# The rows of four RMS norms: column products and a power, or one fp32 product and ScalarE's reciprocal root

## The chip, the cores and the metric

The kernel runs on one core of one Trainium2 chip. The core has TensorE (matrix products, PE in the profile, its weight loads PEld), VectorE (DVE), ScalarE (ACT), GpSimd (POOL) and the queue engine SyncE (SP), which issues most of the transfers. Each engine works through its own queue in order and waits on semaphores. TensorE writes into PSUM, eight banks of 128 partitions by 512 fp32 values; everything else lies in SBUF. The metric is the time of one execution on the device in microseconds (us), as the median of several runs.

## The reference

The program is one decoder layer on 512 tokens of width 1024, all in fp32: a SwiGLU feed-forward block (ffn1), a mixer of state-space heads and differential attention (mix), cross-attention into a memory of 256 tokens (cross), a second feed-forward block (ffn2) and a final norm. What matters here is that each of the four blocks begins with an RMS norm of the 512 tokens:

```python
def rms_norm(x, w):
    x32 = x.astype(jnp.float32)
    y = x32 * lax.rsqrt(jnp.mean(x32 * x32, axis=-1, keepdims=True) + EPS)
    return y.astype(x.dtype) * w

x = x + 0.5 * swiglu(rms_norm(x, norm_ffn1_w[l]), ...)
x = x + hybrid_mixer(rms_norm(x, norm_mix_w[l]), ...)
x = x + memory_cross_attention(rms_norm(x, norm_cross_w[l]), rms_norm(mem, norm_mem_w[l]), ...)
x = x + 0.5 * swiglu(rms_norm(x, norm_ffn2_w[l]), ...)
```

EPS is 1e-6 and the mean runs over 1024 values. So each norm needs, for every token, the reciprocal root of the mean square.

## The kernel before

The state x lies transposed: eight tiles of 128 features (partitions) by 512 tokens (columns). Weights come from memory in tiles of 128 x 1024 (wr, six buffers), and every fp32 operand of a large product is split into a high part (wh, h; ScalarE copies it to the format fp32r) and a low part (wl, l; VectorE subtracts), with three buffers each; a product is then three fp32r products, high by high, high by low, low by high. The two feed-forward blocks also use Strassen-like block products of 256 columns (`quad`, line 252: banks qa, qe, qb). TensorE's queue is therefore a long row of such products, and the splits are what ScalarE and VectorE mostly do.

The norm's factor is per token, that is per column of these tiles. A gain per feature is applied when a tile is split or scaled; the factor per token is multiplied in as a row of 512 values that stands in all 128 partitions. Class `Stat` makes it. `add` squares each of the eight x tiles (ScalarE) and adds them up (VectorE, tile nacc). `finish` (lines 404 to 413) then takes these steps:

- four column products, each with a block of 128 tokens of nacc as weights and a column of ones moving, so that each token's sum lands in a column (tile nps, 128 x 4);
- on VectorE the division by 1024 and EPS (nv), on GpSimd the power -0.5 (ncol, line 379);
- after some microseconds of other TensorE work (`yield apart`), four products that spread the column into a row over all partitions, with the column broadcast as weights and the identity moving (tile nrow);
- a ScalarE copy of that row into SBUF (tile row).

What uses the row: at ffn1 the gate of the first hidden tiles and the scaled tiles fe and fo; at mix eight tiles hf (line 425), each split into hnh and hnl, which all projections of the mixer read, the first being the query product pq; at cross the query tiles cqf (line 1131); at ffn2 the gates (line 453). ffn2 also needs the factor as a column, for tokens on partitions (col4 and ncol4, lines 1385 and 1386).

The order in which instructions are written is set by `Order`: it counts TensorE's time with every product, runs the dense work (generators that yield after each group of products) and puts in side chains when their counted time has come; `finish` is such a chain. SyncE's and GpSimd's queues keep that written order; on the other engines a scheduler may move instructions that do not depend on each other. Around the mix norm the dense work is the memory's keys (bank pck, eight products of 24 steps), at cross the first query products (pcq), at ffn2 the first quad. GpSimd's queue also holds transfers that add one weight tile onto another in memory (isum, wsum), so what stands behind the power there waits for it.

ScalarE keeps one table of functions at a time; a function from another table needs an ACT_TABLE_LOAD first. The kernel before loads four times: at the start, before the first Silu, before the first Exp, and before the Silu of ffn2.

Of the kernel before, what the change touches and what calls it, by code (L numbers as in the profile page):

```python
# [11 lines left out]
F32 = mybir.dt.float32  # L12
# [5 lines left out]
P = 128  # L18
# [81 lines left out]
def body(tc, a, dbg=None):  # L100
# [31 lines left out]
    def aux(s, shape=(P, T)):  # L132
        return aux_p.tile(list(shape), F32, tag="aux", name=nm(s))
# [9 lines left out]
    def mm(out, w, x, start, stop):  # L143
        od.t += (1 if w.dtype == R32 else 4) * (x.free_size() + 8) / 2400
        newest_mm[:] = [nc.tensor.matmul(out, w, x, start=start, stop=stop).ins]  # L145
# [213 lines left out]
    ones = cp.tile([P, P], F32, name="ones")  # L359
    V.memset(ones, 1.0)  # L360
    mhalf = cp.tile([P, 4], F32, name="mhalf")
    S.activation(mhalf, ones[:, :4], AF.Copy, scale=-0.5)
    ones_r = cp.tile([P, P], R32, name="ones_r")
    V.tensor_copy(ones_r, ones)
# [17 lines left out]
    def row_of(col, nb):  # L382
# [3 lines left out]
                mm(pr[:, b * P : (b + 1) * P], col[:, b : b + 1].to_broadcast([P, P]), ident, True, True)  # L386
        return pr

    class Stat:
        def __init__(self, n_tok=T):  # L390
            self.n = n_tok
            self.acc = None
            self.row = None

        def add(self, xk):
            if self.acc is None:
                self.acc = s2("nacc", shape=(P, self.n))
                S.activation(self.acc, xk, AF.Square)
            else:
                sq = s2("nsq", shape=(P, self.n))  # L400
                S.activation(sq, xk, AF.Square)
                V.tensor_tensor(self.acc, self.acc, sq, ALU.add)

        def finish(self, apart=2.5):
            nb = self.n // P
# [11 lines left out]

    def normed(st, c, dst):

        yield from st.finish()  # L420
        hf = {}
        for k in range(KT + 1):
            if k < KT:
                hf[k] = s2("hf")
                V.scalar_tensor_tensor(hf[k], x[k], par[:, c + k : c + k + 1], st.row, ALU.mult, ALU.mult)
            if k > 0:
                dst.append(split("hn", hf.pop(k - 1)))
                yield 1.6
# [139 lines left out]
    start.extend(last)  # L568
    with tc.issue_after(start[0]):
        for k in range(KT):  # L570
            st1.add(x[k])
    st_mix, h = Stat(), []

    def beside(ti):
# [3 lines left out]
            od.spawn(memory_prep(hm, 2.5), 10.0)  # L578

    def fin1(o):  # L580
        st_mix.add(x[o])
        if o == KT - 3:
            od.spawn(normed(st_mix, C_MIX, h), 3.0)
            od.spawn(block_sums_in_dram(), 60.0)

    od.spawn(st1.finish(), 18.0)
    od.add(ffn1(h1, wa_s, fin1, beside))


# [501 lines left out]
    def upd_c(o, po):  # L1091
        V.tensor_tensor(x[o], x[o], po, ALU.add)
        h_c.append(make_h(o, C_CROSS))
        st_c.add(x[o])
        dump(f"x2_{o}", x[o])
        if o == KT - 1:
            h.clear()
            od.spawn(st_c.finish(), 3.0)

    hm, hm2 = [], []  # L1100
    od.add(memory_keys())
# [72 lines left out]
    def upd_2(o, po):  # L1174
        V.tensor_tensor(x[o], x[o], po, ALU.add)
        gain = par[:, C_FFN2 + o : C_FFN2 + o + 1]
        if o % 2:
            h, l = split("hm", x[o], gain)
            half["12"], half["22"] = hl((h, l), slice(0, H)), hl((h, l), slice(H, T))
            xs_2.append(block_sums(o - 1, C_FFN2, dict(half), even.pop()))  # L1180
        else:
            half["11"] = [s2("h11" + p_, R32, (P, H)) for p_ in "hl"]
            split_into(*half["11"], x[o][:, :H], gain)
            even.append(scaled(o, C_FFN2))
        st_2.add(x[o])
# [306 lines left out]
```

## Time and profile before

| | |
|---|---|
| median of 3 runs | 1308.36 us (1307.47 to 1309.42) |
| the profiled execution | 1306.71 us, of it span 1304.7 us |
| granted TensorE clock | 0.998 of full speed |
| TensorE busy | 1292.8 us, 99% of the span |
| VectorE, ScalarE, GpSimd busy | 969.6, 695.3, 108.9 us |
| the norms' first column product starts at | 25.2, 355.6, 849.8, 971.8 us |

The span is what the profiler saw of the program; the execution's own time has some 2 us around it. A row of the timeline gives start, duration, engine, line, operation, the tile written and the tiles read, the shape, the count, and in brackets how long the engine sat idle before it and what ended that. "issue" means that the profile shows no reason. TensorE's matmuls overlap and their ends are modelled, so distances between starts are the better measure there. An fp32 product shows two records, an fp32r product one.

### The profile page before, as it was taken

The page shows a single profiled execution, that of the slowest core. Times are in us where ns is not written, and L with a number is a line of the kernel's source. Part 1 is how long each engine was busy: PE and PEld are TensorE (multiplying, and loading weights), DVE is VectorE, ACT ScalarE, POOL GpSimd, SP SyncE. Part 2 cuts the span into 40 slices and gives each one's busy share as a digit, 9 for nine tenths or more (in the row PEclk, how much of TensorE's full clock was granted, in tenths as well). Part 3 has the DMA queues.
Part 4 walks back from the last instruction along what each step waited for, and adds up shares of the span by engine and source line. Part 5 has one row for each costly group of instructions (what it writes and reads, how often), then busy time and mean ns, then how long its engine had stood idle before and what let it go on. Part 6 is the DMA issues. An engine that isn't in the chain of part 4 may idle for free.

```text
span 1304.7 us, 20807 instructions
## 1 busy us (share of the span) xinstructions
PE 1292.8 (99%) x8108; PEld 1150.9 (88%) x8108; DVE 969.6 (74%) x1520; ACT 695.3 (53%) x1183; POOL 108.9 (8%) x127
## 2 busy tenths in 40 slices
PE   9999999999999999999999999999999999999997
PEld 7889999999987788887888888888899999989995
DVE  6886888788884787548877796656677878877886
ACT  6444654556553666336564564434465645555564
POOL 1010010000010011200101012020011000000001
PEclk9999999999999999999999999999999999999999
DMA  8156667767664434953468379594239875655662
GB/s 310 49 192 170 191 166 196 186 182 195 186 232 151 129 90 118 265 182 93 117 182 246 105 174 260 188 225 143 69 106 253 223 229 168 191 201 172 191 204 91
DMA packets 69729, 229.03 MB, mean 176 GB/s; under 512 B 8616, under 2 KB 12176, under 8 KB 69280
## 3 DMA queue, kind: packets, MB, share of 16 engines
q1 hardware_dynamic: 52832, 176.26, 38.7%
q0 software_dynamic: 13056, 44.65, 18.9%
q10 hardware_dynamic: 3744, 6.82, 1.7%
q8 instruction: 63, 1.03, 0.3%
q14 instruction: 34, 0.28, 0.1%
HBM read 225.53 MB, written 50.91 MB: 212 GB/s over the span
## 4 chain that ended last, share of the span: by engine, by line
PE 90%; issue 6%; DVE 2%; ACT 1%; POOL 1%; POOLq 0%; ACTq 0%; DVEq 0%
PE qb L252 15%; PE pm L145 10%; PE qa L252 10%; PE qe L252 10%; PE pxbc L145 5%; PE pcq L145 3%; PE pz L145 3%; PE po L145 3%; PE ob L1258 3%; PE pv L145 3%; PE oa L1258 2%; PE pq L145 2%; PE oe L1258 2%; PE pk L145 2%; PE pa L145 2%
## 5 line engine op out<-in xcount | busy, mean ns | idle before, releaser
L154 ACT ACTIVATE wh<-wr 128x1024 fp32r<-128x1024 f32 (+2 forms) x323 | 329.3, 1022 | 355.6 <-issue 95.7
L155 DVE TENSOR_TENSOR wl<-wr,wh 128x1024 fp32r<-128x1024 f32 (+2 forms) x323 | 379.7, 1178 | 144.6 <-ACT wh L154 138.6
L145 PE MATMUL pxbc<-hnh,wh 128*128 128x512 f32 x128 | 52.9, 413 | 0.0
L252 PE MATMUL qb<-s24h,wl 128*128 128x256 f32 x184 | 52.2, 284 | 0.2 <-DVE wl L155 0.2
L252 PE MATMUL qb<-s24h,wh 128*128 128x256 f32 x184 | 52.4, 285 | 0.0
L252 PE MATMUL qb<-s24l,wh 128*128 128x256 f32 x184 | 52.2, 284 | 0.0
L252 PE MATMUL qb<-s31h,wh 128*128 128x256 f32 x184 | 52.2, 283 | 0.0
L252 PE MATMUL qe<-s31h,wh 128*128 128x256 f32 x184 | 52.1, 283 | 0.0
L252 PE MATMUL qb<-s31l,wh 128*128 128x256 f32 x184 | 52.1, 283 | 0.0
L252 PE MATMUL qe<-s24l,wh 128*128 128x256 f32 x184 | 52.1, 283 | 0.0
L252 PE MATMUL qe<-s24h,wh 128*128 128x256 f32 x184 | 52.1, 283 | 0.0
L252 PE MATMUL qb<-s31h,wl 128*128 128x256 f32 x184 | 52.1, 283 | 0.0
L252 PE MATMUL qe<-s31l,wh 128*128 128x256 f32 x184 | 52.1, 283 | 0.0
L252 PE MATMUL qe<-s24h,wl 128*128 128x256 f32 x184 | 52.1, 283 | 0.0
L252 PE MATMUL qe<-s31h,wl 128*128 128x256 f32 x184 | 52.1, 283 | 0.0
L145 PE MATMUL pxbc<-hnh,wl 128*128 128x512 f32 x128 | 50.2, 392 | 0.0
L145 PE MATMUL pxbc<-hnl,wh 128*128 128x512 f32 x128 | 49.9, 390 | 0.0
L754 ACT ACTIVATE ec<-ec,mn 128x512 f32<-128x512 f32 (+3 forms) x64 | 35.5, 556 | 25.7 <-DVE mn L753 25.6
L252 PE MATMUL qa<-h11h,wh 128*128 128x256 f32 x152 | 43.1, 283 | 0.0
L252 PE MATMUL qa<-h11h,wl 128*128 128x256 f32 x152 | 43.0, 283 | 0.0
L252 PE MATMUL qa<-h11l,wh 128*128 128x256 f32 x152 | 43.0, 283 | 0.0
L860 DVE SCALAR_TENSOR_TENSOR conv<-pxbc,par,conv 128x511 f32<-128x511 f32 (+2 forms) x48 | 35.8, 746 | 6.5 <-ACT conv L857 5.7
(490 smaller groups left out, 4171.0 us busy)
## 6 DMA issues: line engine op xcount, KB each, us to landing
wr<-in_f2q SPq DMA_DIRECT2D x44, 512.0 KB, 4.2
wr<-in_f1q SPq DMA_DIRECT2D x40, 512.0 KB, 4.5
isum<-in_f2q SPq DMA_DIRECT2D x22, 512.0 KB, 5.3
wr<-isum SPq DMA_DIRECT2D x22, 512.0 KB, 4.2
wr<-in_f1o SPq DMA_DIRECT2D x20, 512.0 KB, 3.9
wsum<-in_f2b SPq DMA_DIRECT2D x20, 512.0 KB, 6.6
wr<-wsum SPq DMA_DIRECT2D x20, 512.0 KB, 4.3
wr<-in_f1q POOLq DMA_DIRECT2D x16, 512.0 KB, 5.7
```

The lines of the kernel that those rows point to most:

```text
L145: newest_mm[:] = [nc.tensor.matmul(out, w, x, start=start, stop=stop).ins]
L154: S.activation(hi, src, AF.Copy),
L155: V.tensor_tensor(lo, src, hi.bitcast(F32), ALU.subtract),
L252: newest_mm[:] = [nc.tensor.matmul(out, a_[:, wc], b_, start=first and f == 0 and kp == 0 and j == 0, stop=kp == n - 1 and j == 2, skip_gr ...
L754: S.activation(ec[:, :n], ec[:, :n], AF.Exp, bias=mn, scale=-1.0, accum_out=sm[c][:, i : i + 1])
L860: V.scalar_tensor_tensor(y[:, d:], ps[:, : T - d], par[:, cw + j : cw + j + 1], y[:, d:], ALU.mult, ALU.add)
L1258: newest_mm[:] = [nc.tensor.matmul(ps, a_[:, ts], b_[:, ws], start=first and k == 0 and j == 0, stop=k == n - 1 and j == 2, skip_group_che ...
```

## The change

For the four norms of 512 tokens the column products, the power and the spreading products go. The memory's norm and the state-space groups' norms keep theirs.

- The sums go with a minus sign: the last `add` of a norm computes -nacc - sq in one three-operand VectorE instruction. (At mix the last tile added is the sixth, since the tiles come in the order 6, 7, 4, 5.)
- `root_row`: one fp32 product with a 128 x 128 tile of ones as weights and nacc moving gives every token's sum as a row in all partitions at once (nps, now 128 x 512). ScalarE takes the reciprocal root of its absolute value (scale and eps_root bring in EPS and the factor; the result is half the wanted one, divided by 1024), then squares it into a second tile. VectorE multiplies this by the sum and then, in the second instruction, completes a Newton step and the factor.
- `finish_row` is that chain. At ffn2 `finish_both` adds, 16 us of counted time later, four transposes of the row and a VectorE copy of one column out of each, which gives the column that col4 and ncol4 are made from.
- At the start one small ScalarE instruction with the reciprocal root stands ahead of the tile mhalf, so that the first table load brings the table with this function.

```diff
+    eps_root = cp.tile([P, 1], F32, name="eps_root")
+    V.memset(eps_root, 4.0 * D * D * EPS)
+    S.activation(mhalf, ones[:, :4], AF.Abs_reciprocal_sqrt)
     S.activation(mhalf, ones[:, :4], AF.Copy, scale=-0.5)
...
+    def root_row(sums, r, w, sign):
+
+        ps = aux("nps")
+        with behind(list(newest_mm)):
+            mm(ps, ones, sums, True, True)
+        S.activation(r, ps, AF.Abs_reciprocal_sqrt, bias=eps_root, scale=4.0 * D * sign)
+        S.activation(w, r, AF.Square, scale=2.0 * D)
+        V.scalar_tensor_tensor(w, ps, sign * D * EPS, w, ALU.add, ALU.mult)
+        V.scalar_tensor_tensor(r, w, -3.0 * D * sign, r, ALU.add, ALU.mult)
+
...
-        def add(self, xk):
+        def add(self, xk, last=False):
...
-                V.tensor_tensor(self.acc, self.acc, sq, ALU.add)
+                if last:
+                    V.scalar_tensor_tensor(self.acc, self.acc, -1.0, sq, ALU.mult, ALU.subtract)
+                else:
+                    V.tensor_tensor(self.acc, self.acc, sq, ALU.add)
+
+        def finish_both(self, apart):
+            yield from self.finish_row()
+            yield apart
+            nb = self.n // P
+            pt = aux("pcol")
+            for b in range(nb):
+                transpose(pt[:, b * P : (b + 1) * P], self.row[:, b * P : (b + 1) * P])
+            self.col = small("ncol", nb, bufs=6)
+            V.tensor_copy(self.col, pt.rearrange("p (a b) -> p a b", b=P)[:, :, 0])
+
+        def finish_row(self):
+            self.row = s2("row")
+            root_row(self.acc, self.row, s2("nsq"), -1)
+            yield 0.0
...
     def normed(st, c, dst):
 
-        yield from st.finish()
+        yield from st.finish_row()
...
-        st_mix.add(x[o])
+        st_mix.add(x[o], o == KT - 3)
...
-    od.spawn(st1.finish(), 18.0)
+    od.spawn(st1.finish_row(), 18.0)
...
-            od.spawn(st_c.finish(), 3.0)
+            od.spawn(st_c.finish_row(), 3.0)
...
-            od.spawn(st_2.finish(8.0), 7.5)
+            od.spawn(st_2.finish_both(16.0), 7.5)
```

On TensorE the change stands in the same places as the column products did. At ffn1 (pa are the first four hidden tiles, hm the scaled x) the queue holds before:

```order
L145 MATMUL pa_280<-hmh_194,wal_199 128x512
L145 MATMUL nps_365<-ones,nacc_210 128x1 x4
L145 MATMUL pa_277<-hmh_202,wah_206 128x512
L145 MATMUL pa_277<-hml_203,wah_206 128x512
L145 MATMUL pa_277<-hmh_202,wal_207 128x512
```

and with the change:

```order
L145 MATMUL pa_283<-hmh_197,wal_202 128x512
L145 MATMUL nps_370<-nacc_213,ones 128x512
L145 MATMUL pa_280<-hmh_205,wah_209 128x512
L145 MATMUL pa_280<-hml_206,wah_209 128x512
L145 MATMUL pa_280<-hmh_205,wal_210 128x512
```

Four one-column products became one of 512 columns at the same place; the nrow x4 that stood twelve rows further, ahead of the first pg, is gone. The same holds for the other three norms; at ffn2 four pcol transposes are new, within the second quad's first block product.

On VectorE at mix (hf are the scaled tiles, hnl their low parts, wl the low parts of the weights, wdts a small tile) the queue holds before:

```order
L377 TENSOR_SCALAR nv_4098<-nps_4093 128x4
L155 TENSOR_TENSOR wl_4218<-wr_4215,wh_4217 128x1024
L425 SCALAR_TENSOR_TENSOR hf_4140<-x_79,par,row_4138 128x512
L425 SCALAR_TENSOR_TENSOR hf_4142<-x_79,par,row_4138 128x512
L155 TENSOR_TENSOR hnl_4145<-hf_4140,hnh_4144 128x512
L425 SCALAR_TENSOR_TENSOR hf_4157<-x_80,par,row_4138 128x512
L155 TENSOR_TENSOR wl_4254<-wr_4251,wh_4253 128x1024
L155 TENSOR_TENSOR hnl_4160<-hf_4142,hnh_4159 128x512
L425 SCALAR_TENSOR_TENSOR hf_4184<-x_80,par,row_4138 128x512
L648 TENSOR_TENSOR wdts_4456<-wdt_4454,wdts_4456 128x8x16
L155 TENSOR_TENSOR wl_4297<-wr_4294,wh_4296 128x1024
```

and with the change, behind the first Newton pass (nsq) and wdts, which stand ahead of these rows:

```order
L400 SCALAR_TENSOR_TENSOR row_4088<-nsq_4089,row_4088 128x512
L456 SCALAR_TENSOR_TENSOR hf_4096<-x_79,par,row_4088 128x512
L456 SCALAR_TENSOR_TENSOR hf_4098<-x_79,par,row_4088 128x512
L155 TENSOR_TENSOR wl_4253<-wr_4250,wh_4252 128x1024
L155 TENSOR_TENSOR hnl_4101<-hf_4096,hnh_4100 128x512
L456 SCALAR_TENSOR_TENSOR hf_4119<-x_80,par,row_4088 128x512
L155 TENSOR_TENSOR hnl_4122<-hf_4098,hnh_4121 128x512
L456 SCALAR_TENSOR_TENSOR hf_4147<-x_80,par,row_4088 128x512
L155 TENSOR_TENSOR hnl_4150<-hf_4119,hnh_4149 128x512
L456 SCALAR_TENSOR_TENSOR hf_4174<-x_81,par,row_4088 128x512
L155 TENSOR_TENSOR wl_4288<-wr_4285,wh_4287 128x1024
```

The third weight split of these rows (wl_4297 before, wl_4288 now) moved behind one more hf and one more hnl, and two Newton passes stand ahead of all of it.

On ScalarE at ffn2 (qa, qe, qb are the quad's banks, p and u copies of them, gate the first gated tile) the queue holds before:

```order
L298 ACTIVATE qb_10094<-qa_10092 128x512
L306 ACTIVATE p_2030_10161<-qe_10093 128x512
L154 ACTIVATE wh_10223<-wr_10087 128x1024
L154 ACTIVATE wh_10262<-wr_10090 128x1024
L314 ACTIVATE u_2033_10192<-qb_10094 128x512
L154 ACTIVATE wh_10290<-wr_10085 128x1024
L413 ACTIVATE row_10255<-nrow_10250 128x512
L154 ACTIVATE wh_10343<-wr_10327 128x1024
L454 ACT_TABLE_LOAD
L454 ACTIVATE gate_10319<-gate_10319 128x512
```

and with the change:

```order
L298 ACTIVATE qb_10073<-qa_10071 128x512
L154 ACTIVATE wh_10201<-wr_10066 128x1024
L397 ACT_TABLE_LOAD
L397 ACTIVATE row_10131<-nps_10133,eps_root 128x512
L398 ACTIVATE nsq_10132<-row_10131 128x512
L306 ACTIVATE p_2024_10139<-qe_10072 128x512
L314 ACTIVATE u_2027_10170<-qb_10073 128x512
L154 ACTIVATE wh_10233<-wr_10069 128x1024
L154 ACTIVATE wh_10261<-wr_10064 128x1024
L485 ACT_TABLE_LOAD
L485 ACTIVATE gate_10290<-gate_10290 128x512
```

Table load, root and square stand ahead of the copies p and u, and the split wh of the fourth product (wh_10262 before, wh_10233 now) moved behind u. Table loads are eight in all instead of four: one more at mix, two more at cross (one ahead of the root, one ahead of the next Exp) and one more at ffn2.

More of the change, by code (lines that the diff above doesn't have):

```diff
@@ L570, in body @@
         for k in range(KT):
-            st1.add(x[k])
+            st1.add(x[k], k == KT - 1)
     st_mix, h = Stat(), []
@@ L1093, in upd_c @@
         h_c.append(make_h(o, C_CROSS))
-        st_c.add(x[o])
+        st_c.add(x[o], o == KT - 1)
         dump(f"x2_{o}", x[o])
@@ L1184, in upd_2 @@
             even.append(scaled(o, C_FFN2))
-        st_2.add(x[o])
+        st_2.add(x[o], o == KT - 1)
         dump(f"x3_{o}", x[o])
```

## Prediction, made before the changed kernel was run

> **What bounds the kernel now.** I read the page first (busy shares and chain), then the waits by engine, then the timeline around the four norms.
>
> ```profile
> span 1304.7 us, 20807 instructions
> PE 1292.8 (99%) x8108; PEld 1150.9 (88%) x8108; DVE 969.6 (74%) x1520; ACT 695.3 (53%) x1183; POOL 108.9 (8%) x127
> ...
> PE 90%; issue 6%; DVE 2%; ACT 1%; POOL 1%; POOLq 0%; ACTq 0%; DVEq 0%
> ...
> PE ptk L149 <- ACT of L810: 0.6, 1, 0.6
> ```
>
> TensorE works 99% of the span and makes 90% of the chain that ends last; in the list of waits its longest after the start is 0.6 us. So nearly every microsecond taken off TensorE's queue comes off the end, and work on the other engines is free until it makes TensorE wait. The change has to be priced as TensorE's time first, and as the lateness of what TensorE reads second. I call the four norms by their stages: ffn1, mix, cross, ffn2.
>
> **What is taken off TensorE.** Around the ffn1 norm:
>
> ```profile
> 25.20 0.94 PE L145 MATMUL nps<-ones,nacc 128*128 128x1 f32 x8
> ...
> 26.33 0.40 PE L145 MATMUL pa<-hml,wah 128*128 128x512 f32 x1
> ...
> 28.64 0.39 PE L145 MATMUL pa<-hmh,wal 128*128 128x512 f32 x1
> 28.87 1.05 PE L145 MATMUL nrow<-ident,ncol 128*128 128x128 f32 x8
> 29.68 0.48 PE L145 MATMUL pg<-hmh,wh 128*128 128x512 f32 x1
> 29.99 0.39 PE L145 MATMUL pg<-hml,wh 128*128 128x512 f32 x1
> ```
>
> The durations are modelled, so I go by starts. A plain 512-column product takes 0.23 (28.64 to 28.87). The four column products hold the queue from 25.20; the second product behind them starts at 26.33, so they cost 26.33 - 25.20 - 0.23 = 0.90. The four products that spread the column into a row cost 29.99 - 28.87 - 0.23 = 0.89. Both go: 1.79 a norm.
>
> **What is put in.** One fp32 product, ones as weights, 512 columns moving. The trace has none of this shape. Two rows bound it: the four spreading products above also stream 4 x 128 fp32 columns against 128-row weights, in 0.81 by starts (29.68 - 28.87) and 0.89 with what follows; the other is two fp32 products of 256 columns with 32-row weights:
>
> ```profile
> 71.36 1.02 PE L145 MATMUL prel<-hot,rel_sb 32*8 32x256 f32 x4
> 72.32 0.50 PE L145 MATMUL pu<-hmh,wh 128*128 128x512 f32 x1
> 72.66 0.39 PE L145 MATMUL pu<-hml,wh 128*128 128x512 f32 x1
> ```
>
> That is 72.66 - 71.36 - 0.23 = 1.07. I take 0.90, because the weights have 128 rows as in the first; the ends are 0.81 and 1.07. A norm then saves 1.79 - 0.90 = 0.89.
>
> Two corrections. At mix and at cross TensorE already waits for the sums:
>
> ```profile
> 355.56 0.97 PEld L145 LDWEIGHTS nps<-ones,nacc 128*128 128x128 f32 x8 [0.31 <-DVE nacc L402]
> ...
> 849.47 0.39 PE L145 MATMUL pcq<-hmh,wh 128*128 128x512 f32 x1
> 849.82 1.02 PE L145 MATMUL nps<-ones,nacc 128*128 128x1 f32 x8
> ```
>
> (0.31, and 0.35 instead of 0.23.) The last addition becomes a three-operand instruction, some 0.06 dearer (steps of 0.67 against 0.60, the hf and hnl rows below), and TensorE waits that much longer: 0.83 each. At ffn2 the old products were partly cover for another wait:
>
> ```profile
> 964.30 1.91 PE L149 MATMUL pxf<-ident,x 128*128 128x128 f32 x16
> 965.97 0.36 PE L252 MATMUL qa<-h11h,wh 128*128 128x256 f32 x1
> ...
> 971.80 0.95 PE L145 MATMUL nps<-ones,nacc 128*128 128x1 f32 x8
> 972.76 0.39 PE L252 MATMUL qb<-s24h,wh 128*128 128x256 f32 x1
> ...
> 972.13 0.58 ACT L298 ACTIVATE qb<-qa 128x512 f32<-128x512 f32 x1
> ```
>
> The product behind them starts at 972.76, when ScalarE's copy into its bank is done (972.13 + 0.58 = 972.71). So there the shorter product gains nothing; only the spreading goes, 0.89, and four transposes come for the columns: 16 took 965.97 - 964.30 = 1.67, so four take 0.42, with the change-over some 0.45. Net 0.44.
>
> TensorE's sum: 0.89 + 0.83 + 0.83 + 0.44 = 2.99. With the product at 1.07 it is 2.3, at 0.81 it is 3.3.
>
> **What is added beside it.** Each norm gets two ScalarE passes (root, square) for one copy, and two VectorE passes of 0.74 for one small instruction and GpSimd's power; ScalarE loads its function table four times more in all. Where is that covered?
>
> ```profile
> 30.57 1.28 ACT L434 ACT_TABLE_LOAD   x1
> 31.87 0.63 ACT L434 ACTIVATE gate<-gate 128x512 f32<-128x512 f32 x1
> ...
> 354.47 1.06 ACT L154 ACTIVATE wh<-wr 128x1024 fp32r<-128x1024 f32 x1 [0.31 <-ACT nsq L401]
> 358.60 1.06 ACT L154 ACTIVATE wh<-wr 128x1024 fp32r<-128x1024 f32 x1 [3.07 <-PE pck L145]
> ...
> 852.65 1.06 ACT L154 ACTIVATE wh<-wr 128x1024 fp32r<-128x1024 f32 x1 [4.37 <-issue]
> ```
>
> A load is 1.28. At mix it falls into ScalarE's idle 3.07 before 358.60, at cross into the 4.37 before 852.65, both while the sums are still under way: no cost. Were that idle gone, each would delay the row by 1.28. At ffn2 the load, root and square stand between two weight splits and the two copies of the running product; the second copy keeps its place, because one split that stood ahead of it now stands behind. The Trainium skill, "ScalarE: Activation LUTs", section "What ACT_TABLE_LOAD costs", adds a drain of about 1.38 us to each 1.283 us load. Here the next activation starts 0.02 after the load, so the trace shows the load alone; by the page's figure mix and ffn2 would lose an estimated 0.2 each and the sum below would be 2.4 instead of 2.8.
>
> At cross ScalarE's order puts a weight copy (852.65) between root and square, so square starts at 853.7 and the two VectorE passes, behind a weight split, end at 856.4 to 856.6. There the first query tile is scaled:
>
> ```profile
> 855.03 0.69 DVE L1131 TENSOR_TENSOR cqf<-pcq,row 128x512 f32<-128x512 f32 x1
> 859.19 0.69 DVE L1131 TENSOR_TENSOR cqf<-pcq,row 128x512 f32<-128x512 f32 x1 [2.08 <-PE pcq L145]
> ```
>
> Some 1.5 later than 855.03, but the second waits for its product at 859.19 anyway: covered. At ffn2 the row now comes before two of the weight splits. The split that matters, wl of the fourth product, moves from 977.45 to about 978.3, and its first user stands at 982.37, 0.9 earlier with the spreading gone: 2 us are left.
>
> ```profile
> 977.45 1.22 DVE L155 TENSOR_TENSOR wl<-wr,wh 128x1024 fp32r<-128x1024 f32 x1
> ...
> 982.37 0.28 PE L252 MATMUL qe<-s24h,wh 128*128 128x256 f32 x1
> ```
>
> **The narrow place is mix,** where VectorE has no idle:
>
> ```profile
> 359.69 1.23 DVE L155 TENSOR_TENSOR wl<-wr,wh 128x1024 fp32r<-128x1024 f32 x1 [2.83 <-ACT wh L154]
> 360.91 1.41 DVE L425 SCALAR_TENSOR_TENSOR hf<-x,par,row 128x512 f32<-128x512 f32 x2
> ...
> 366.03 0.28 DVE L648 TENSOR_TENSOR wdts<-wdt,wdts 128x128 fp32r<-128x128 f32 x1
> 366.33 1.23 DVE L155 TENSOR_TENSOR wl<-wr,wh 128x1024 fp32r<-128x1024 f32 x1
> ...
> 376.12 1.29 DVE L155 TENSOR_TENSOR hnl<-hf,hnh 128x512 fp32r<-128x512 f32 x2
> ...
> 376.63 0.40 PE L145 MATMUL pq<-hnh,wh 128*128 128x512 f32 x1
> ```
>
> Back to back, a three-operand pass takes 0.67 (1.41 for two), an hnl 0.60. In the new order the two Newton passes and wdts stand ahead of hf, so hf starts at 360.92 + 2 x 0.67 + 0.28 = 362.54, 1.6 later. The last hnl, 377.41 before, then ends between 378.4 and 379; the query product reads it 7 x 0.68 + 0.23 after its start, 381.6, or 380.7 with TensorE 0.89 earlier: covered. The weight split that stood at 366.33 now has seven three-operand passes, three hnl, wdts and one split ahead of it: 360.92 + 4.69 + 1.80 + 0.28 + 1.23 = 368.92, and ends at 370.15. Its product is two before the query's, 2 x 2.88 (24 steps of 0.12) before 376.63, so at 370.87, now 369.98; it reads the lo part two steps in, 370.22. Nothing is spare. If every step is as quick as counted TensorE waits not at all; if each of the 13 is 0.08 slower it waits 1.0. I take 0.2, near the counted end.
>
> **Sum:** 2.99 - 0.2 = 2.8 less. The profiled execution took 1306.71 (span 1304.7), so it would take 1303.9. The median of the three runs, 1308.36, lies 1.65 above it; with the same 2.8 the time is 1305.6. Own range of this case: from 2.31 - 1.0 = 1.3 to 3.3 less, 1305.1 to 1307.1.
>
> **Rivals.**
> VectorE becomes the bound at mix: the split comes 1.0 late and the lead of 0.89 is given back: 2.99 - 1.9 = 1.1 less, 1307.3. For it: the zero spare time. Against: the count uses 1.23 for a split although the next instruction may start sooner.
>
> The fp32 product is dear (the slower side). No row has 512 fp32 columns in one instruction. If that streams at half the pace of the nearest costly row, 2 x 1.07 = 2.14, each of the four norms pays 1.24 more than I counted, 5.0 in all: 2.8 less becomes 2.2 more, 1310.6. It decides from 0.90 + 2.8 / 4 = 1.6 a product. For it: from 4 x 128 to 2 x 256 columns the price already rose from 0.89 to 1.07. Against: that row also differs in its 32-row weights.
>
> GpSimd's transfers are no rival of their own:
>
> ```profile
> 851.13 1.03 POOL L379 TENSOR_TENSOR ncol<-nv,mhalf 128x4 f32<-128x4 f32 x1 [38.33 <-DVE nv L377]
> 852.14 3.40 POOL L1228 DMA_DIRECT2D isum<-in_f2q  x4
> ```
>
> The power waited 38.33 at the head of its queue; without it the four transfers behind can start sooner, among the weight loads. But raw weights lie six tiles deep, and a product takes 24 x 0.23 = 5.4, so a load has some 27 us until its split. Their cover is that depth; I cost them at nothing.
>
> **Chances.** A difference below 0.2%, 2.6 us, cannot be told from no change here. Forecast 0.75, VectorE at mix 0.16, dear product 0.09. Within the forecast two parts in three lie beyond 2.6: faster 0.51. The rest of it, the VectorE rival and a small part of the dear product, whose gain or loss can stay under 2.6, give same 0.43; the rest of the dear product is slower, 0.06. The range goes from 1304.2 (3.3 less, and 0.9 as the lowest run lies below the median) to 1308.4, which takes in the VectorE rival.
>
> **What would show it.** Each norm has one nps record group of about 0.9 and no nrow; the next product's start after it tells the price. TensorE's list of waits stays without wl at mix (right) or names wl L155 near 370 (VectorE rival). The forecast is wrong if the span falls by less than 1.3, or if the product takes over 1.1.

## The result, and the profile after

The changed kernel takes 1302.82 us (median of 6 runs, 1302.48 to 1303.10), the kernel before in the same comparison 1307.91 (6 runs, 1307.06 to 1309.42): a ratio of 0.9959, 95% interval [0.9946, 0.9971], 5.1 us less. The prediction said 1305.6 and 1304.2 to 1308.4: the direction was right, the gain was taken too small by 2.3, and the time lies below the range. (One run of the kernel before, in the comparison of e9 to e12 below, took 3282.39 us; it is in no median here.) One thing is visible before any trace is opened: the six runs of the kernel before spread over 2.4 us, those of the changed kernel over 0.6.

The head of the page of the changed kernel:

```profile
span 1300.7 us, 20708 instructions
...
PE 1288.8 (99%) x8056; PEld 1145.3 (88%) x8056; DVE 974.8 (75%) x1526; ACT 704.1 (54%) x1192; POOL 103.9 (8%) x123
```

Span 4.0 less, TensorE's busy time 4.0 less, VectorE's 5.2 and ScalarE's 8.8 more: the gain is work off TensorE, and the work added elsewhere did not show. TensorE's list of waits says the same; apart from the start it still has only these two, and no weight split at mix:

```profile
PE ptk L149 <- ACT of L841: 0.6, 1, 0.6
PE qb L252 <- DVE wl L155: 0.2, 1, 0.2
```

The norm of ffn1 in TensorE's timeline, to be held against the rows of before (25.20 to 29.99):

```profile
24.92 1.02 PE L145 MATMUL nps<-nacc,ones 128*128 128x512 f32 x2
25.37 0.79 PE L145 MATMUL pa<-hmh,wah 128*128 128x512 f32 x1
26.00 0.39 PE L145 MATMUL pa<-hml,wah 128*128 128x512 f32 x1
...
28.31 0.39 PE L145 MATMUL pa<-hmh,wal 128*128 128x512 f32 x1
28.54 0.39 PE L145 MATMUL pg<-hmh,wh 128*128 128x512 f32 x1
28.77 0.39 PE L145 MATMUL pg<-hml,wh 128*128 128x512 f32 x1
```

The fp32 product costs 26.00 - 24.92 - 0.23 = 0.85 where the prediction had 0.90, and behind the last pa comes pg at once, without the four spreading products.

**Where the 4.0 us of the two traces lie.** I laid the starts of TensorE's products of both traces side by side and noted where their distance changes. ffn1 gives 0.94, mix 0.95, cross 0.93, ffn2 0.43 (0.88 for the spreading, 0.45 back for the four transposes): 3.25. The rest is not the norms': 0.28 at the start (the second group of pa starts at 6.75 instead of 7.03, where the first input transfers land a little differently in each execution) and 0.42 late in ffn2, most of it one wait at 1252 us. The profiled execution of before (1306.71) is also one of its quicker ones. So the two traces account for 4.2 of run time (4.0 of span, and 0.2 around it), the medians for 5.1. The missing part cannot be in these two traces; it must be in executions of the kernel before that were longer than the profiled one. That was the first question for the runs.

### The profile page after: what moved, and what is told of

Its sections match the earlier page's. It is cut to its first block, busy times and chain, and to the rows that moved or that the text cites. A ratio compares the mean times of both kernels' runs of the same rounds, so it can differ in the third digit from the quotient of the medians.

```text
span 1300.7 us, 20708 instructions
## 1 busy us (share of the span) xinstructions
PE 1288.8 (99%) x8056; PEld 1145.3 (88%) x8056; DVE 974.8 (75%) x1526; ACT 704.1 (54%) x1192; POOL 103.9 (8%) x123
## 4 chain that ended last, share of the span: by engine, by line
PE 90%; issue 6%; DVE 2%; ACT 1%; POOL 1%; POOLq 0%; ACTq 0%; DVEq 0%
PE qb L252 15%; PE pm L145 10%; PE qa L252 10%; PE qe L252 10%; PE pxbc L145 5%; PE pz L145 3%; PE pcq L145 3%; PE po L145 3%; PE ob L1289 3%; PE pv L145 3%; PE oa L1289 2%; PE pq L145 2%; PE oe L1289 2%; PE pk L145 2%; PE pa L145 2%
```

## The experiments

Times are medians in us, with the lowest and highest run. All runs of a group shared a chip with runs of the kernel before. The changed kernel itself was timed only in the comparison above. Four of the kernels below, which only add an unused power or one or two small copies to it (e2, e10, e15, e16), gave 1302.62 to 1302.94 in other comparisons; so differences to the 1302.82 hold to some 0.2.

### What a product costs: e4_product_twice

```diff
-            mm(ps, ones, sums, True, True)
+            for _ in range(2):
+                mm(ps, ones, sums, True, True)
```

> The change, with the fp32 product of ones with the sums issued twice in a row into the same bank, for the four norms: its price by itself. By the step between starts in the changed kernel's trace, 0.85 to 0.90 each, the time rises by 2.6 (ffn2's second may partly cover a wait) to 3.6 us. By the dear price that one rival of the prediction assumed, 2.14 each, by 8.6 us.

1306.01 (1305.72 to 1306.28; 11 runs), 3.2 over the changed kernel, as expected, or 0.80 on average for the four further products. The average hides a difference: laid beside the changed kernel's trace, TensorE's products move back by 0.85 at mix, 0.86 at cross and 0.66 at ffn2, where the second product covers a part of a wait, as the expectation allowed. (At ffn1 executions differ by up to 0.6 on their own.) So the price is 0.85, and the dear product (from 1.6 on) is ruled out.

### Is the scatter real, and where is it: e1_before_again

The kernel before, unchanged, as a kernel of its own.

> The kernel before, unchanged, to see how far its own executions lie apart. If the 5.1 us between the medians are all TensorE's queue, its executions repeat within 0.5 us as those of the change do (1302.5 to 1303.1) and lie near 1307.9. If about 1 us of the difference is a second, longer course that the kernel before takes in some executions, they fall into two groups, near 1307.1 and near 1309.3, and the profile's TensorE waits differ from the first profile's at the start, at 113 us or near 1252 us.

1307.77 (1305.96 to 1311.05; 11 runs), beside 1307.39 for the 27 runs of the kernel before in the same comparison; ratio 1.0001 [0.9992, 1.0010]. The scatter of 3 us and more belongs to the program, but it is not the two groups that the expectation described: the eleven runs lie all along the way from 1306 to 1309 and one beyond. Nor is the wait below at one of the three places that it named. By luck the profiled execution was a long one, span 1307.6. Side by side with the profiled execution of before, TensorE is 0.75 later from the start, gains and loses little until 1000 us, drops back by some 0.8 up to 1021, and then loses 1.57 at one product. There is the wait, with the ScalarE row that begins it (timeline of the long execution):

```profile
1017.99 1.06 ACT L154 ACTIVATE wh<-wr 128x1024 fp32r<-128x1024 f32 x1 [3.58 <-DMA wr<-in_f2q]
...
1019.08 1.22 DVE L155 TENSOR_TENSOR wl<-wr,wh 128x1024 fp32r<-128x1024 f32 x1 [3.30 <-ACT wh L154]
...
1026.70 0.68 DVE L325 TENSOR_TENSOR c<-p,qb 128x512 f32<-128x512 f32 x1
...
1027.53 0.36 PE L252 MATMUL qb<-hmh,wh 128*128 128x256 f32 x1 [1.42 <-DVE c L325]
```

The same places in the shorter profiled execution of before:

```profile
1014.70 1.06 ACT L154 ACTIVATE wh<-wr 128x1024 fp32r<-128x1024 f32 x1 [1.64 <-DMA wr<-in_f2q]
...
1023.41 0.68 DVE L325 TENSOR_TENSOR c<-p,qb 128x512 f32<-128x512 f32 x1
...
1024.34 0.28 PE L252 MATMUL qb<-hmh,wh 128*128 128x256 f32 x1
```

How to read it: in the second quad of ffn2 a weight tile is the sum of two (one transfer loads, a second one of GpSimd's adds). ScalarE waits for that sum, VectorE's split behind it is late, and from 1019 on VectorE works without a gap until c, the last instruction that reads the bank qb. TensorE may write that bank only then. In the short execution the sum came 1.64 late, c was done at 1024.09, and TensorE, due at 1024.34, did not notice. At 3.58 it stood for 1.42. So the kernel before ran with 0.25 us to spare at that place, and what varies is when a weight sum lands: from GpSimd's issue to landing the addition took 7.2 in the short execution (issued at 1007.38) and 9.0 in the long one (1008.88).

Not all of the scatter is this. The long execution took 1311.05, 3.45 more than its span. In the changed kernel and the kernels made from it (e2, e4 to e6, e10 to e16) a run is 1.72 to 1.85 longer than its span; in the kernel before and those made from it (e1, e3, e7 to e9) it is 1.72 to 3.63 longer, in the median of the kernel before 1.85 to 1.96. No profile here shows what lies outside the span, so this part stays open.

### Which part of the old norm makes the sum late

Six runs take the old norm apart. First GpSimd's power alone, in both directions.

e2_pool_wait puts the power back into the changed kernel, at its old place in the queue, with a result that nothing uses:

```diff
+        v = small("nv", 4)
+        V.tensor_scalar(v, ps[:, 0:4], -1.0 / D, EPS, ALU.mult, ALU.add)
+        G.tensor_tensor(small("ncol", 4, bufs=6), v, mhalf, ALU.pow)
```

> The change, with a GpSimd power (its result unused) put back at the place in GpSimd's queue where the norms' power stood, waiting for the new product. Nothing else moves. Theory one, TensorE's queue alone: as the change, 1302.8 within 0.3, since TensorE's rows stay. Theory two, GpSimd's queue: the transfers behind the power are held back again, and the time rises by 1.0 to 1.5 us, to some 1304, with executions that lie up to 2 us apart.

1302.62 (1302.23 to 1303.21; 5 runs): no cost, no scatter.

e3_act_root takes the power out of the kernel before at all four norms: ScalarE's reciprocal root on the 128 x 4 columns takes its place, without a Newton step, so with less precision; column and spreading products stay. As in the change, a small root at the start brings the function table with it:

```diff
+    S.activation(mhalf, ones[:, :4], AF.Abs_reciprocal_sqrt)
...
-            G.tensor_tensor(col, v, mhalf[:, :nb], ALU.pow)
+            if own:
+                S.activation(col, v, AF.Abs_reciprocal_sqrt)
+            else:
+                G.tensor_tensor(col, v, mhalf[:, :nb], ALU.pow)
```

> The kernel before, with the four norms' power on 128 x 4 values taken from GpSimd and done as ScalarE's reciprocal root (no Newton step, so the factor is less exact); column products, spreading and copy stay. Theory one: TensorE's rows stay, so the time is that of the kernel before, 1307.9 within 0.5. Theory two: GpSimd's queue is free, and the time falls by about 1 us or its long executions go.

1306.40 (1305.80 to 1307.30; 11 runs) beside 1307.39; ratio 0.9994 [0.9985, 1.0003]. The interval reaches past 1, but the scatter shrinks from 3.4 to 1.5. If that is real, the two runs disagree: the power does something in the kernel before and nothing in the changed one. So I cut by norm.

e7_act_at_ffn2 and e8_act_at_three are e3 with `own` true at ffn2 only, and at the other three only.

> The kernel before with ScalarE's reciprocal root of the 128x4 columns in place of GpSimd's power at ffn2's norm alone (no Newton step, so the root has less precision; products as before). Theory GpSimd's queue at ffn2: the same as with all four on ScalarE, 1306.4, executions within 1.6 us. Theory TensorE's queue alone, or that the place is another norm: as the kernel before, 1307.4, executions over 2.5 us apart.

> The kernel before with ScalarE's reciprocal root of the 128x4 columns in place of GpSimd's power at the norms of ffn1, mix and cross (no Newton step there), GpSimd's power kept at ffn2. Theory GpSimd's queue at ffn2: as the kernel before, 1307.4, executions over 2.5 us apart. If another norm's power is the cause: 1306.4, executions within 1.6 us.

e5_ffn2_old is the changed kernel with the old norm at ffn2, e6_ffn2_new the kernel before with the new norm at ffn2 alone:

```diff
-        st_2.add(x[o], o == KT - 1)
+        st_2.add(x[o])
...
-            od.spawn(st_2.finish_both(16.0), 7.5)
+            od.spawn(st_2.finish(8.0), 7.5)
```

(e5; e6 puts back the calls of the other three norms in the same way.)

> The change with ffn2's norm put back in its old form (four column products, GpSimd's power, four spreading products, apart 8.0); the norms of ffn1, mix and cross stay new. What is open is why the long executions of the kernel before lose 2.4 us between 1000 and 1028 us, where ScalarE waits 3.58 us for a weight sum, and why the changed kernel has no such executions. Theory TensorE's queue alone: ffn2's norm is worth its 0.43 us of products and the 0.42 us behind it, so 1303.3 to 1303.7, executions within 1.2 us. Theory GpSimd's queue at ffn2: the power holds back the issue of a 512 KB weight sum, so the scatter of the kernel before comes back whole: median 1304.3 to 1305.2, executions over 2.5 us apart.

> The kernel before with ffn2's norm alone changed; the norms of ffn1, mix and cross keep column products, GpSimd's power and spreading products. Theory TensorE's queue alone: 0.44 to 0.85 under the kernel before, so 1306.6 to 1307.1, executions still over 2.5 us apart if the scatter is not ffn2's. Theory GpSimd's queue at ffn2: the scatter goes too, 1305.2 to 1305.8, executions within 1.6 us.

All four ran on one chip, 11 runs each, the kernel before at 1307.55 (33 runs, 1306.45 to 1310.07):

| kernel | median (lowest to highest) | ratio [95% interval] |
|---|---|---|
| e7, no power at ffn2 | 1306.26 (1305.70 to 1307.97) | 0.9990 [0.9981, 0.9999] |
| e8, no power at the other three | 1307.57 (1306.88 to 1309.33) | 1.0000 [0.9991, 1.0008] |
| e6, new norm at ffn2 alone | 1305.78 (1305.17 to 1306.69) | 0.9987 [0.9978, 0.9996] |
| e5, new norm at the other three | 1305.00 (1302.86 to 1305.55) | 0.9975 [0.9966, 0.9983] |

All four medians came out where the theory of GpSimd's queue at ffn2 put them, or within 0.2. The place is ffn2: the power there costs 1.3 us, at the three others nothing. (e7's highest run, 1307.97, breaks the 1.6 that was expected of its spread, but its span is an ordinary 1304.4; the spans of e7 lie within 1.1, those of the kernel before within 3.9.) ffn2's norm as a whole, forecast at 0.44, is worth 1.8 in the kernel before and 2.2 in the changed one. And e5's runs fall into two groups, five from 1302.9 to 1304.2 and six from 1305.0 to 1305.6, as a stall of some 1.5 us that comes in about half of the executions would make them. Both e5 and e8 were profiled with the stall, and in both the ScalarE row ahead of it has a wait above 3 us. ScalarE's timeline in e5:

```profile
1013.82 1.06 ACT L154 ACTIVATE wh<-wr 128x1024 fp32r<-128x1024 f32 x1 [3.52 <-DMA wr<-in_f2q]
```

and in e8:

```profile
1016.28 1.06 ACT L154 ACTIVATE wh<-wr 128x1024 fp32r<-128x1024 f32 x1 [3.21 <-DMA wr<-in_f2q]
```

### The transfer behind the power: e9_wsum_first

What stands behind the power in GpSimd's queue at ffn2? GpSimd's timeline in the kernel before:

```profile
947.02 0.89 POOL L260 DMA_DIRECT2D wr<-in_f2q  x1 [75.81 <-DVE s31l L155]
973.11 1.89 POOL L379 TENSOR_TENSOR ncol<-nv,mhalf 128x4 f32<-128x4 f32 x1 [25.20 <-DVE nv L377]
974.97 0.89 POOL L1228 DMA_DIRECT2D wsum<-in_f2b  x1
988.16 0.89 POOL L260 DMA_DIRECT2D wr<-in_f2q  x1 [12.29 <-DVE wl L155]
```

The power waits 25.20 us for its sums, and a transfer of 512 KB into a weight sum in DRAM (wsum), which needs none of this, waits behind it. In the changed kernel's timeline that transfer leaves at once:

```profile
943.75 0.89 POOL L260 DMA_DIRECT2D wr<-in_f2q  x1 [82.56 <-DVE s31l L155]
944.32 1.18 POOL L1259 DMA_DIRECT2D wsum<-in_f2b  x1
```

e9 is the kernel before with that one transfer issued ahead of the power. The side chain that issues the transfers yields once for no time and once for double the time; the queues of TensorE, VectorE and ScalarE stay as they were. (One of SyncE's copies into a later sum, which the same step of the chain issues, moved up in SyncE's queue with it; the text below takes it for the copy of the same sum. In e7 that copy stays where it was.)

```diff
+                left = len(jobs) + LEAD - n
-                yield 8.0
+                yield 8.0 - 8.0 * (left == 8) + 8.0 * (left == 7)
```

> The kernel before with one change of order: at ffn2 the 512 KB transfer that adds to a weight sum in DRAM (and the copy that fills that sum, two places earlier in SyncE's queue) is issued ahead of the norm's power in GpSimd's queue, not behind it; power, column products, spreading products and VectorE's queue stay. The stall looked for is the one of 1.5 us at the qb products at about 1024 us, seen in two of three long executions of kernels with GpSimd's power at ffn2. Theory held transfer: the stall goes and with it the scatter, 1306.0 to 1306.5, executions within 1.6 us (as with ScalarE's root at ffn2, 1306.26). Theory VectorE's wait (its copy of the columns waits 0.93 us for the power, and the split behind it): as the kernel before, 1307.5, executions over 2.5 us apart.

1306.27 (1305.84 to 1306.86; 11 runs) beside 1307.67 for the kernel before (16 runs); ratio 0.9990 [0.9981, 0.9999]. The scatter is down to 1.0 and the median is within 0.01 of e7's. The power is still there, and VectorE still waits 0.93 for its result; only the transfer and that copy moved (timelines of GpSimd and ScalarE in e9):

```profile
947.15 1.19 POOL L1228 DMA_DIRECT2D wsum<-in_f2b  x1
972.81 1.89 POOL L379 TENSOR_TENSOR ncol<-nv,mhalf 128x4 f32<-128x4 f32 x1 [24.48 <-DVE nv L377]
983.66 0.93 POOL L260 DMA_DIRECT2D wr<-in_f2q  x1 [8.96 <-DVE gate L453]
...
1014.10 1.06 ACT L154 ACTIVATE wh<-wr 128x1024 fp32r<-128x1024 f32 x1 [1.33 <-PE qe L252]
```

ScalarE's split at 1014 no longer waits for a transfer. The DMA views of the stretch from 972 to 990 us show what the held transfer did (issues: count, size, median us from issue to landing). In the kernel before:

```profile
wr<-in_f2q SPq DMA_DIRECT2D x4, 512.0 KB, 7.8
```

and in e9:

```profile
wr<-in_f2q SPq DMA_DIRECT2D x4, 512.0 KB, 4.8
```

Held to 975, it runs among the loads of the quad's weights; these take 7.8 us instead of 4.8, and the addition onto one of them is issued at 988.16 instead of 983.66. Issued at 947 it lies ahead of them. That addition makes a weight sum, and ScalarE's split of the sum waits for it in the kernel before, in e9 not at all (ScalarE's timeline in the kernel before):

```profile
995.95 1.06 ACT L154 ACTIVATE wh<-wr 128x1024 fp32r<-128x1024 f32 x1 [3.27 <-DMA wr<-in_f2q]
```

From there the times follow one another: VectorE works off its queue without a gap from 997 to 1011, SyncE's next three loads go out at 1000.36 (998.36 in e9), the next addition at 1007.38 (1006.13), and the split at 1014.70 is the one that waits for it. So this one transfer's place in a queue is worth 1.4 us of the median here (1.3 by e7) and most of the scatter. Both intervals reach from 0.1 to 2.5 us, so the size is rough; by the medians of the spans it is 1.0 (e9) and 1.2 (e7).

### Why does the changed kernel stand the same hold

In e2 the transfer is held as long as before (issued at 971.6) and nothing happens. Two theories: VectorE's own wait for the power is needed too, which e2 left out, or the hold is not yet long enough.

e10_pool_read adds to e2 one VectorE copy of the power's result at ffn2, where the kernel before read it; e11_pool_hold puts four more powers behind the first one instead:

```diff
...
+        if read:
+            V.tensor_copy(small("pcopy", 4), p)
...
```

```diff
...
+        if read:
+            for _ in range(4):
+                q = small("phold", 4)
+                G.tensor_tensor(q, p, mhalf, ALU.pow)
+                p = q
...
```

> The change with GpSimd's power put back at the norms' places (as in the run with the power's wait, result not used in the output), and at ffn2 one VectorE copy of its 128x4 result right where the kernel before read it, so that VectorE waits for the power too. Theory held transfer: as without that copy, 1302.6, executions within 1.0 us. Theory VectorE's wait: the stall comes back in a part of the executions, median 1303.2 to 1304.6, executions over 1.5 us apart.

> The change with GpSimd's power put back and, at ffn2, four more powers behind it (none used), so that the 512 KB transfer queued behind them is issued 4 to 7 us later than with one power (975 to 979 us in place of 971.6); nothing on VectorE waits for them. Theory held transfer: what one power did not yet do in the changed kernel this must: the stall of 1.5 us appears, median 1303.6 to 1304.6. Theory VectorE's wait: 1302.6, executions within 1.0 us.

e10: 1302.88 (1302.64 to 1303.23; 5 runs). This run does not put VectorE's wait back, though. In its trace the power ends at 971.85, and the copy, behind a weight split, starts at 972.01 without idle time. That VectorE's wait is not the cause rests on e9 alone, where the wait is still there and the scatter gone. e11: 1303.30 (1302.65 to 1304.22; 5 runs), with the transfer issued at 977.6. That is 0.4 over e10 with a wider spread, but its profiled execution has no stall in ffn2 and loses its time elsewhere (0.36 at the start, 0.38 near 413), so it decides nothing.

e13_hold_late and e14_late make VectorE late at that place by four copies of 0.60 each, with the hold and without; e15_hold_late1 and e16_late1 do the same with one copy:

```diff
...
+        if read:
+            late = s2("nsq")
+            for _ in range(4):
+                V.tensor_copy(late, ps)
...
```

> The change with GpSimd's power put back at the norms' places, and at ffn2 four VectorE copies of the 128x512 product (results not used) between the weight splits behind it, about 2.4 us, as much as VectorE idles there in the kernel before (1.56 and 0.93 us). If it takes a held transfer and a late VectorE together: the stall comes back, 1303.8 to 1305, executions over 1.5 us apart, and more than in e14. If the hold does nothing in this kernel even so: as e14 within 0.3 us.

> The change with the four VectorE copies at ffn2 alone, no power on GpSimd. If it takes both: 1302.8 to 1303.2, executions within 1.0 us. If VectorE's lateness alone makes the stall: as e13, 1303.8 to 1305.

> The change with GpSimd's power put back at the norms' places and one VectorE copy of the 128x512 product at ffn2 (0.6 us, not used). If a held transfer and a late VectorE make the stall together: 1303.3 to 1304.6, executions over 1.5 us apart, at least 0.5 us over e16. If not: within 0.3 us of e16.

> The change with one VectorE copy at ffn2 alone, no power on GpSimd. If there is slack for it: 1302.7 to 1303.1. If VectorE is the narrow place there: 1303.3 to 1303.6, with the hold too.

e13 1309.62 (1309.07 to 1311.52) and e14 1309.96 (1309.63 to 1310.47; 11 runs each): 7 us slower with the hold or without, so another mechanism took over. The four copies moved the weight splits, ScalarE waited for them with the norm's root behind, and its copy u, on which the next qb product rests, came 6.9 later (timeline of e14):

```profile
976.35 1.06 ACT L154 ACTIVATE wh<-wr 128x1024 fp32r<-128x1024 f32 x1 [1.87 <-DVE wl L155]
977.42 1.28 ACT L401 ACT_TABLE_LOAD   x1
978.72 0.69 ACT L401 ACTIVATE row<-nps,eps_root 128x512 f32<-128x512 f32 x1
...
980.45 0.59 ACT L314 ACTIVATE u<-qb 128x512 f32<-128x512 f32 x1
...
981.09 0.58 PE L252 MATMUL qb<-s31h,wh 128*128 128x256 f32 x1 [4.71 <-ACT u L314]
```

TensorE stood for 4.71 us, and the rest of the 7 is its clock (below). e15: 1302.94 (1302.43 to 1303.37), e16: 1302.82 (1302.64 to 1302.86; 5 runs each). Within 0.3 of each other and of the changed kernel: hold and a VectorE 0.6 late do not make the stall either.

So this stays open. What the traces show beside it: in e2 the hold does act, the four loads land after 6.3 us and ScalarE waits 2.15 for a sum at 991.78, but TensorE does not notice. And SyncE issues those loads earlier than with the old norm at ffn2 (e5 has the same first three norms as e2). SyncE's queue in e2:

```profile
972.98 5.29 SPq L258 DMA_DIRECT2D wr<-in_f2q  x3
```

and in e5:

```profile
974.79 3.81 SPq L258 DMA_DIRECT2D wr<-in_f2q  x3
```

That is 1.8 us earlier, 1.4 when TensorE's own 0.4 between these two executions is taken off: about as long as the stall. The next addition then goes out at 1002.19 and takes 7.2, so that it lands 1.4 ahead of ScalarE's split at 1010.80. A second difference stands ahead of it: with the old norm VectorE's s31l and two further small sums stand behind the split of the first late sum, with the new one ahead of it, where VectorE would idle. VectorE's queue in e5:

```profile
994.33 1.23 DVE L155 TENSOR_TENSOR wl<-wr,wh 128x1024 fp32r<-128x1024 f32 x1 [3.03 <-ACT wh L154]
995.47 0.69 DVE L155 TENSOR_TENSOR s31l<-s,s31h 128x512 fp32r<-128x512 f32 x1
```

and in e2:

```profile
989.77 0.68 DVE L155 TENSOR_TENSOR s31l<-s,s31h 128x512 fp32r<-128x512 f32 x1
...
992.88 1.23 DVE L155 TENSOR_TENSOR wl<-wr,wh 128x1024 fp32r<-128x1024 f32 x1 [1.62 <-ACT wh L154]
```

Either could be the reason, or both; neither was tried.

### How much VectorE has to spare at mix: e12_mix_three

```diff
         yield from st.finish_row()
+        w = s2("nsq")
+        for _ in range(3):
+            V.tensor_tensor(w, st.row, st.row, ALU.mult)
         hf = {}
```

> The change with three VectorE passes of 128x512 (0.60 us each from one to the next) put ahead of the first scaled chunk at mix, results not used. By the changed kernel's trace the weight split there ends 368.55 and TensorE needs it at 368.94. Theory that 0.39 us is all the slack there: plus 1.4 us, 1304.2. Theory that something else is narrower or VectorE catches up: 1302.8 to 1303.2.

1303.59 (1303.41 to 1303.99; 5 runs), 0.8 over the changed kernel for 1.8 us of VectorE work: neither the 1.4 of the first theory nor nothing. By its trace TensorE loses 1.07 between 379 and 394, at products that read hnl and ql and at

```profile
PE pdt L145 <- DVE ql L159: 0.4, 1, 0.4
```

and nothing at the weight split. But the split itself moved: the scheduler put the passes between the first scaled tiles and the split ahead of two of the hf and two of the hnl that it stood behind, so that it starts at 367.01, no later than without the passes. The run therefore does not measure the split's slack. It shows that VectorE's queue as a whole, in this order, had about 0.7 to 1.0 us to spare at mix, and that the low parts were then late first.

## Why the prediction was right and wrong, point by point

**TensorE bounds the kernel, its queue is the price: right.** The spreading products were put at 0.89 and gave 0.88 to 0.89 at all four norms.

**The fp32 product, 0.90: the term was a little too large.** 0.85 by starts, and 0.85 to 0.86 by repetition where nothing covers it; the nearer row, the four spreading products (0.81 to 0.89), had been the right one to follow.

**The later sums at mix and cross, 0.06 each: wrong.** The three-operand addition took 0.69, as the plain one does. The row that the 0.06 was taken from, hf, also reads a column of par, and took 0.74 to 0.75; the trace of before had a three-operand pass without such a column, th<-c,gate, at 0.68. With both corrections the four norms gave 3.25 in the traces where the step had 2.99. By runs, e6 against the changed kernel, ffn1, mix and cross together gave 2.96 (2.82 by starts).

**ffn2's queue, 0.44: right.** 0.43 by starts, and 0.49 between e9 and e6, which differ in the norm's form but have the transfer free in both.

**Mix, 0.2 lost: nothing is lost, and the count was right to 0.34.** The split was reckoned to end at 370.15 with its need at 370.22, in the times of the kernel before. Timeline of the changed kernel, in which everything just ahead of mix already lies 1.26 earlier (the start and ffn1):

```profile
358.40 1.22 DVE L155 TENSOR_TENSOR wl<-wr,wh 128x1024 fp32r<-128x1024 f32 x1 [2.87 <-ACT wh L154]
...
360.35 0.68 DVE L400 SCALAR_TENSOR_TENSOR row<-nsq,row 128x512 f32<-128x512 f32 x1
361.07 1.41 DVE L456 SCALAR_TENSOR_TENSOR hf<-x,par,row 128x512 f32<-128x512 f32 x2
362.40 1.22 DVE L155 TENSOR_TENSOR wl<-wr,wh 128x1024 fp32r<-128x1024 f32 x1
...
367.33 1.22 DVE L155 TENSOR_TENSOR wl<-wr,wh 128x1024 fp32r<-128x1024 f32 x1
```

In the times of before, hf starts at 362.33 (reckoned 362.54), and the split, done at 368.55, at 369.81. TensorE came to its product at 368.94, in those times 370.20. So the need came out as reckoned and the split 0.34 earlier: a split takes 1.14 from its start to the next one's where the count had 1.23, as the prediction had said it might, and wdts 0.21 for 0.28. The 0.2 was a reserve that was not needed. The rival in which VectorE becomes the bound there falls by this; its price was also too high, since the need at 370.22 already held the lead of 0.89, and a split 1.0 late would have cost 1.0, not 1.9.

**The table load at cross hidden ahead of the sums: wrong, without cost.** It was not done early but waited with the activation behind it:

```profile
848.78 1.28 ACT L397 ACT_TABLE_LOAD   x1 [2.71 <-PE nps L145]
850.07 0.69 ACT L397 ACTIVATE row<-nps,eps_root 128x512 f32<-128x512 f32 x1
...
854.33 0.69 DVE L1162 TENSOR_TENSOR cqf<-pcq,row 128x512 f32<-128x512 f32 x1
...
856.33 0.68 DVE L1162 TENSOR_TENSOR cqf<-pcq,row 128x512 f32<-128x512 f32 x1
```

It was still covered: the first query tile is scaled at 854.33, the second, whose product comes 2.9 earlier than before, at 856.33, and no wait of TensorE names the row. That a load waits is no rule: at 27.34 and 862.33 in the same trace the loads ran 0.98 and 0.59 ahead of activations that waited for something else. At the other places the load takes 1.28 and the next activation follows within 0.01 to 0.02, as before. The drain that the Trainium skill ("ScalarE: Activation LUTs", "What ACT_TABLE_LOAD costs") adds is not seen here either; the sum of 2.4 that its figure gave is further off than 2.8.

**GpSimd's transfers, costed at nothing: this is the step that failed.** It looked at cross, where the power stands ahead of four transfers, and argued that raw weights lie six tiles deep. Both were beside the point. At cross the hold is indeed free (e8), but at ffn2 the same power holds one transfer into the busiest stretch, and what comes late there is not a plain load but a sum, a load and then an addition onto it, with no depth left: ScalarE already waited for such sums in the profiled execution (3.27 at 995.95, 1.64 at 1014.70). Those rows were in the trace of before and were not read, since TensorE's own list of waits showed nothing at that place. What it was worth: 1.3 to 1.4 us of the median, 1.0 to 1.2 of the span. Why the changed kernel does not suffer from the same hold stays open.

**The base.** The 2.8 were taken off the median of three runs, 1308.36, with the note that the profiled run lay 1.65 below it. The note was the clue: a kernel whose runs lie 2 us apart has something in it that varies, and the change could take that away too. Over the later comparisons the median of before was 1307.4 to 1308.3.

The account of the 5.1: 2.96 for three norms (e6 to the changed kernel), 0.49 for ffn2's queue (e9 to e6), 1.3 to 1.4 for the transfer (before to e7 and to e9); together 4.8 to 4.9. These are steps from median to median along one row of kernels, so that they add up is no evidence; the first two have the traces beside them (2.82 and 0.43), the third only the runs. The 0.2 to 0.3 that are left are within what medians of such runs can tell, and 0.1 to 0.2 of the whole lie outside the span.

## What to carry to other kernels

When runs of a kernel lie further apart than the effect looked for, find out what varies before pricing a change: one profiled execution shows only one side of it, and the waits of the other engines for transfers show how near the edge it is. On a queue that works in order, look at what stands behind an instruction that waits: a power of 2 us that waited 25 held back a transfer that needed nothing from it, and moving that transfer alone gave over a quarter of what the whole change gave. Price work on the bounding engine from the nearest row of the same shape; that part of the forecast came within 10%.

## What the runs showed of the hardware

**A pause of 4.71 us cost TensorE another 2.** In e14 TensorE stood for 4.71 us. The windows behind it (us; busy time and count of TensorE, its loads, VectorE, ScalarE, GpSimd; granted clock; share and rate of the transfers):

```profile
976.00:981.00 5.00, 0.38 (x4) 0.17 (x2) 2.97 (x5) 4.59 (x6) 0.30 (x1) 0.73 0.83 252
981.00:985.00 4.00, 3.91 (x18) 3.91 (x19) 1.71 (x3) 1.95 (x3) 2.27 (x3) 0.50 1.02 269
985.00:989.00 4.00, 4.00 (x35) 4.00 (x35) 1.98 (x3) 1.25 (x2) 0.00 (x0) 0.98 1.05 203
```

For 4 us the granted clock was 0.50, and 18 products ran where 35 run at full clock: 2 us more lost. In e13, with the same pause, the clock was 0.51 from 980 to 984. In the long execution of e1 the pause was 1.42, and the window behind it kept 1.00:

```profile
1026.00:1030.00 4.00, 2.58 (x22) 2.51 (x22) 3.11 (x5) 0.63 (x1) 0.00 (x0) 1.00 1.04 267
```

The Trainium skill ("TensorE: Matmul & The Clock Gate", "What's actually happening") puts the step to half the clock at an idle window of about 3.4 us; a pause of 4.71 with it and one of 1.42 without it agree.

**One fp32 product of 512 columns costs no more than four of one column.** 0.85 against 0.90 for the four column products, each of which loads 128 rows of weights for a single column.
